# State-space stage of a hybrid trunk: three output tiles as one group, and more filling ahead of the decay products

## The chip, the cores and the metric

The kernel runs on one core of a Trainium2 chip. The metric is the device time of one execution in microseconds. The engines of the core are TensorE (PE; its weight loads are PEld), VectorE (DVE), ScalarE (ACT), GpSimd (POOL) and SyncE (SP); each works through its own queue in order, and semaphores join them. TensorE's accumulators lie in PSUM, everything else on the chip in SBUF.

## What is computed

One inference step of two layers on 384 tokens (128 of a prompt, 256 latent ones) with 1024 features, in float32. Layer 0 mixes tokens by state-space heads (SSD) and gated delta heads side by side, then a ConvFFN; layer 1 by spatial gating and windowed attention, then another. The change lies in layer 0's mixer. Of its reference this matters:

```python
def ssd_scan(x, dt, A, Bm, Cm, h0):              # chunks of 128 tokens
    acs = jnp.cumsum(dtc * A.astype(F32), axis=2)
    seg = acs[:, :, :, None, :] - acs[:, :, None, :, :]
    lmat = jnp.exp(jnp.where(tril, seg, -jnp.inf))                 # decay
    xdt = xc * dtc[..., None]
    scores = jnp.einsum('bcihn,bcjhn->bcijh', cc, bc) * lmat
    y_diag = jnp.einsum('bcijh,bcjhp->bcihp', scores, xdt)
    chunk_states = jnp.einsum('bcjhn,bcjh,bcjhp->bchpn', bc, decay_to_end, xdt)
    y_off = jnp.einsum('bcihn,bchpn,bcih->bcihp', cc, h_prev, jnp.exp(acs))
...
y = rmsnorm(y.reshape(bsz, length, SSD_INNER) * jax.nn.silu(z.astype(F32)), ssd_norm_w)
...
mixed = jnp.concatenate([y, o.reshape(bsz, length, DN_V)], axis=-1).astype(h.dtype)
return mixed @ w_out
```

`o` is the delta heads' output, `w_out` the output projection of both.

## The kernel before

**Matmuls in two halves.** Every projection is done with a high and a low half of each operand: ScalarE casts a high half (`whi` of a weight at L345, `oh`, `hh` of an activation at L371), and VectorE or GpSimd subtracts it from the source to make the low half (`wlo` at L348, `ol`, `hl` at L372). A tile of 128 output features takes eight contraction rows k and three matmuls for each (high by high, low by high, high by low), 24 in all. `Net.group` (L393, L395) and `Net.acc` (L378 to L380) write them, the latter in one order for each k and without a loop over tiles. Four PSUM banks serve these tiles. Weights come in an order planned beforehand, through three landing buffers `wst` and six pairs of halves.

**Weaving.** The mixer's scans have little matmul work between long chains on the other engines. So they are written as generators that yield a pair (TensorE's work just issued, the time to wait before the next piece), and `weave` fills the time to wait with pieces of another generator, the filling: it keeps a clock that adds up the planned work, in units of about a microsecond, and takes filling as long as no scan is due. In the delta stage (some 70 to 145 us) the filling is projection tiles. In the state-space stage (some 380 to 530 us) it is first the eight tiles of the SSD input (`fill_x`), with a convolution of five taps on ScalarE (L696) and VectorE (L700), transposes back to tokens (L728), and then the output projection's delta half, `fill_o`; after each of its pieces comes a piece of a modulation "quad" (L301, L308). The compiler's scheduler can shift instructions on each engine; dependences hold.

**Decay.** `decay` makes the exponentials of the sums `seg` for four heads at a time by matmuls (L818) of a triangle with products `er` of a mask and the factors, high half on VectorE, low half on GpSimd (both L809). Pairs of products are made `deep` steps ahead; then a wait of 2.0 units is yielded before the first matmul. `ner`, the number of `er` buffers, is 4 in the state-space stage and 5 in the delta stage, so that `deep` is 2 in both. The buffers also hold the tiles `m` of L1134 and L1135.

**State-space chunk.** For each of three chunks and two halves of the heads: decay; `G` by matmul (L1122), masked to `GU`, `GL` (L1129, VectorE); for each of eight heads a scaled copy on ScalarE (L1134) and a multiply-add on VectorE (L1135); the product with the decay (L1138, VectorE); the state's part (L1150, L1156 to L1160); the output matmuls (L1168, L1171); skip term and gate `z` (L1176, L1177, VectorE; `z` is loaded by GpSimd's queue at L1174), a square on ScalarE (L1179) and its sums (L1183). Beside them run the chunk states: `BT` transposed (L1214), copied (L1217), `xd` made on VectorE (L1221), multiplied (L1225) and added (L1237) or copied out (L1230, through a buffer shared with `z`).

**`fill_o`** splits the delta output (eight casts L371 on ScalarE, eight subtractions L372 on GpSimd), then makes one tile after another with `group`; the copy of a tile to `part` is on ScalarE. `HOLD` = 2 of its pieces are kept for behind the weave.

## Time and profile before

| | |
|---|---|
| three timed runs | 1443.51, 1444.91, 1444.94 us |
| median | 1444.91 us |
| profiled execution, its own time | 1436.85 us |
| its span in the trace | 1435.1 us |
| mean granted clock of TensorE | 0.983 |
| TensorE busy | 1368.8 us (95%) |
| VectorE busy | 929.1 us (65%) |
| ScalarE busy | 791.1 us (55%) |
| GpSimd busy | 196.6 us (14%) |

The profiled execution is one of its own, and all times within the trace are told from its span's start. Durations of single instructions come from it; its own time is what they add up against.

### The profile page before, as it was taken

How to read it: one execution, taken by the hardware profiler on the slowest of the kernel's cores; microseconds unless marked ns; L12 is line 12 of the kernel's file. 1: busy time of each engine (PE TensorE's matmuls, PEld its weight loads, DVE VectorE, ACT ScalarE, POOL GpSimd, SP SyncE). 2: the span in 40 equal slices, each digit the busy share in tenths (PEclk: the TensorE clock that was granted, in tenths of full speed). 3: DMA queues.
4: the chain of work that ended last, by engine and by line, in shares of the span. 5: the costliest groups of instructions: out<-in, count | busy, mean ns of one | idle time of the engine just before them, and what ended most of it. 6: DMA issues, size and time to landing. Idle time of an engine off the chain costs nothing.

```text
span 1435.1 us, 26679 instructions
## 1 busy us (share of the span) xinstructions
PE 1368.8 (95%) x10421; PEld 1297.3 (90%) x10421; DVE 929.1 (65%) x1819; ACT 791.1 (55%) x1757; POOL 196.6 (14%) x189
## 2 busy tenths in 40 slices
PE   5989998999999999899999999999999899999996
PEld 3889897998887789899999998989999899999996
DVE  3586994755889766776676445466667586776432
ACT  3568567668575435655454445454855465555431
POOL 0023011012345304200000113000003300000001
PEclk9999999999999999999999999999999999999998
DMA  9334544302743475645534442544234344344441
GB/s 345 136 117 135 180 156 146 129 29 80 226 150 105 144 243 176 235 136 162 175 119 125 121 125 71 173 145 134 75 118 154 126 120 131 121 129 121 129 122 55
DMA packets 60334, 201.61 MB, mean 140 GB/s; under 512 B 7120, under 2 KB 12000, under 8 KB 60208
## 3 DMA queue, kind: packets, MB, share of 16 engines
q1 hardware_dynamic: 52832, 186.25, 40.8%
q10 hardware_dynamic: 6048, 8.93, 1.7%
q0 software_dynamic: 1328, 4.73, 1.1%
q8 instruction: 82, 1.34, 0.4%
q14 instruction: 44, 0.36, 0.1%
HBM read 191.20 MB, written 8.68 MB: 139 GB/s over the span
## 4 chain that ended last, share of the span: by engine, by line
PE 82%; DVE 8%; POOL 3%; DMA 3%; ACT 2%; issue 2%; SPq 0%; POOLq 0%; DVEq 0%; ACTq 0%
PE mm L393 19%; PE mm L378 11%; PE mm L379 11%; PE mm L380 11%; PE mm L395 10%; PE pmod L301 3%; DVE wlo L348 1%; PE ps L498 1%; DMA wst<-w 1%; POOL er L809 1%; PE mmt L1552 1%; PE ps L1627 1%; PE mmt L1553 1%; PE mmt L1554 1%; POOL xres L564 1%
## 5 line engine op out<-in xcount | busy, mean ns | idle before, releaser
L348 DVE TENSOR_TENSOR wlo<-wst,whi 128x512 fp32r<-128x512 f32 (+1 forms) x497 | 345.5, 700 | 204.5 <-ACT whi L345 199.4
L345 ACT CAST whi<-wst 128x512 fp32r<-128x512 f32 (+1 forms) x505 | 304.6, 613 | 287.9 <-PE mm L379 157.4
L393 PE MATMUL mm<-hh,whi 128*128 128x386 f32 x728 | 247.1, 339 | 6.7 <-ACT hh L371 5.8
L393 PE MATMUL mm<-hh,wlo 128*128 128x386 f32 x728 | 244.8, 336 | 0.0
L395 PE MATMUL mm<-hl,whi 128*128 128x386 f32 x728 | 238.6, 338 | 0.3 <-DVE hl L372 0.2
L378 PE MATMUL mm<-hh,whi 128*128 128x386 f32 x552 | 194.9, 353 | 1.7 <-ACT t L1343 1.5
L379 PE MATMUL mm<-hl,whi 128*128 128x386 f32 x552 | 189.2, 343 | 0.9 <-issue 0.9
L380 PE MATMUL mm<-hh,wlo 128*128 128x386 f32 x552 | 188.5, 342 | 0.6 <-DVE wlo L348 0.6
L393 PEld LDWEIGHTS mm<-hh,whi 128*128 128x128 f32 x728 | 136.8, 188 | 9.3 <-ACT hh L371 6.4
L395 PEld LDWEIGHTS mm<-hl,whi 128*128 128x128 f32 x728 | 136.1, 188 | 1.5 <-DVE hl L372 1.4
L393 PEld LDWEIGHTS mm<-hh,wlo 128*128 128x128 f32 x728 | 136.9, 188 | 0.0
L378 PE MATMUL mm<-gh,whi 128*128 128x386 f32 x352 | 119.5, 339 | 0.0
L379 PE MATMUL mm<-gl,whi 128*128 128x386 f32 x352 | 119.3, 339 | 0.0
L380 PE MATMUL mm<-gh,wlo 128*128 128x386 f32 x352 | 118.9, 338 | 0.0
L378 PEld LDWEIGHTS mm<-hh,whi 128*128 128x128 f32 x552 | 104.9, 190 | 9.0 <-issue 4.2
L598 DVE SCALAR_TENSOR_TENSOR t<-mm,vecs,t 128x385 f32<-128x385 f32 x88 | 54.3, 619 | 84.5 <-ACT t L597 84.5
L379 PEld LDWEIGHTS mm<-hl,whi 128*128 128x128 f32 x552 | 105.0, 190 | 1.9 <-issue 1.5
L380 PEld LDWEIGHTS mm<-hh,wlo 128*128 128x128 f32 x552 | 104.5, 189 | 1.0 <-DVE wlo L348 0.9
L700 DVE SCALAR_TENSOR_TENSOR t<-mm,vecs,t 128x384 f32<-128x384 f32 (+1 forms) x152 | 92.2, 611 | 14.1 <-ACT t L694 10.0
L597 ACT ACTIVATE t<-mm,vecs 128x386 f32<-128x386 f32 x88 | 58.9, 673 | 69.7 <-PE mm L395 69.7
L520 POOL TENSOR_TENSOR sums<-sums,t 128x386 f32<-128x386 f32 x36 | 41.4, 1172 | 336.8 <-DVE t L517 280.5
L378 PEld LDWEIGHTS mm<-gh,whi 128*128 128x128 f32 x352 | 66.5, 189 | 0.0
(434 smaller groups left out, 2581.9 us busy)
## 6 DMA issues: line engine op xcount, KB each, us to landing
wmod<-modw_l SPq DMA_DIRECT2D x96, 512.0 KB, 4.4
wst<-up_l SPq DMA_DIRECT2D x88, 512.0 KB, 3.5
wst<-w SPq DMA_DIRECT2D x56, 512.0 KB, 3.8
wst<-wo SPq DMA_DIRECT2D x32, 512.0 KB, 3.9
wst<-down_l SPq DMA_DIRECT2D x32, 512.0 KB, 3.5
wst<-w1f SPq DMA_DIRECT2D x18, 512.0 KB, 3.8
wst<-down_l SPq DMA_DIRECT2D x16, 384.0 KB, 3.1
wst<-w1t SPq DMA_DIRECT2D x10, 512.0 KB, 3.7
```

What stands on the lines that cost most here:

```text
L301: nc.tensor.matmul(acc[32 * c:32 * c + 32, 0:128], self.cond[:, k, :], w[:, o:o + 128], start=(k == 0), stop=(k == 7), tile_position=(0, 3 ...
L345: self.conv_hi = nc.scalar.copy(out=hi[:, 0:m], in_=st[:, o:o + m])
L348: self.conv_lo = eng.tensor_sub(out=lo[:, 0:m], in0=st[:, o:o + m], in1=hi[:, 0:m].bitcast(F32))
L378: mm(ps, wh, xh, start=start, stop=False)
L379: mm(ps, wh, xl, start=False, stop=False)
L380: return mm(ps, wl, xh, start=False, stop=stop)
L393: mm(ps, w[k // 4][p][:, s], hh[:, k, :], start=(k == 0 and p == 0), stop=False)
L395: mm(ps, w[k // 4][0][:, s], hl[:, k, :], start=False, stop=(k == 7))
L520: (nc.gpsimd if i else v).tensor_add(out=acc[:, i, :], in0=acc[:, i, :], in1=p)
L597: nc.scalar.activation(out=cv, in_=ps, func=AF.Identity, scale=cw(1), bias=self.v(f"ffb_l{l}", n))
L598: stt(out=cv[:, 1:T], in0=ps[:, 0:T - 1], scalar=cw(0), in1=cv[:, 1:T], op0=ALU.mult, op1=ALU.add)
L700: nc.vector.scalar_tensor_tensor(out=o, in0=p, scalar=cw(i), in1=o, op0=ALU.mult, op1=ALU.add)
```

## The change

Three edits. In `decay`, `deep` is written as 2 (it was 2 in both stages already), and the wait ahead of the first matmul is 5.0 units instead of 2.0, in the three decays of the delta stage and the six of the state-space stage. `ner` of the state-space stage is 5 instead of 4. In `fill_o` the first three tiles are made together with `acc`: k is the outer loop and the tiles the inner one, with a yield of 1.6 units after each k, and the copies of these tiles come when all are done; the number of pieces taken inside the weave goes from 8 to 13 less `HOLD`, which leaves the same tiles for behind it. As pieces are smaller, quad pieces come closer together.

```diff
--- before.py
+++ after.py
@@ -798,7 +798,7 @@
     def decay(self, out, c, col, nh):
         net, nc = self.n, self.nc
         steps = [(b, d) for b in range(nh // 4) for d in range(2)]
-        deep = self.ner // 2
+        deep = 2
 
         def factors(b, d):
             m = net.c(("le", "ge")[d]).unsqueeze(1).to_broadcast([128, 4, 128])
@@ -810,7 +810,7 @@
             return rs
 
         rs = [factors(*s) for s in steps[:deep]]
-        yield 0.0, 2.0
+        yield 0.0, 5.0
         for j, (b, d) in enumerate(steps):
             if d == 0:
                 ps = net.ps()
@@ -1254,7 +1254,7 @@
         end()
         endb, self.hb = net.open("hb", 2)
         end, self.w = net.open("ssd", 1)
-        self.ner = 4
+        self.ner = 5
         out_tile = self.ssd(A)
         end()
 
@@ -1480,9 +1480,17 @@
             for n in range(8):
                 net.split(oh[:, n, :], ol[:, n, :], oT[:, n, :], nc.gpsimd)
             part.append(A("part"))
+            ws = [net.wload(t["wo0"][n, :, 0:1024], 2 - n) for n in range(3)]
+            pss = [net.mm() for _ in ws]
+            for k in range(8):
+                for ps, w in zip(pss, ws):
+                    net.acc(ps, w, k, oh[:, k, :], ol[:, k, :], k == 0, k == 7)
+                yield 1.6
             for n in range(7):
-                nc.scalar.copy(out=part[0][:, n, :], in_=net.group([t["wo0"][n, :, 0:1024]], oh, ol)[0])
-                yield 3.9
+                ps = pss[n] if n < 3 else net.group([t["wo0"][n, :, 0:1024]], oh, ol)[0]
+                nc.scalar.copy(out=part[0][:, n, :], in_=ps)
+                if n > 2:
+                    yield 3.9
             part.append(net.ps()[:, 0:T])
             open_tile(part[1], net.wload(t["wo0"][7, :, 0:1024]), oh, ol, True)
             yield 3.9
@@ -1503,7 +1511,7 @@
         work = [self.ssd_chunk(c, BT, CT, xD, xtok, S) for c, S in
                 ((0, None), (2, (s1[0], s0[1])), (1, (s0[0], s1[1])))]
         rest = fill_o()
-        fill = mix(chain(self.fill_x(), itertools.islice(rest, 8 - HOLD)), chain(net.quads(0, range(8, 12), net.wst), net.quads(1, range(Q0, Q2), net.wst)), 1)
+        fill = mix(chain(self.fill_x(), itertools.islice(rest, 13 - HOLD)), chain(net.quads(0, range(8, 12), net.wst), net.quads(1, range(Q0, Q2), net.wst)), 1)
         weave([late(g, d) for g, d in zip([states()] + work, DS)], fill, W0[3])
         drain(fill, rest)
         part, hold = part
```

How this moves instructions is seen in their order on each engine. Numbers behind names tell tiles apart and are not the same in both programs; words in brackets are the engines waited for.

**First place: the start of `fill_o` (about 436 us in the trace of before), TensorE and ScalarE.** TensorE before, from the last modulation matmuls into the first output tile:

```order
L301 MATMUL pmod_5165<-wmod_5550,cond_83 32x128 [waits DMAHW1_49]
L301 MATMUL pmod_5165<-wmod_5550,cond_83 32x128 x7
L393 MATMUL mm_5596<-oh_5567,whi_5183 128x386 [waits Activation_49]
L393 MATMUL mm_5596<-oh_5567,wlo_5184 128x386
L395 MATMUL mm_5596<-ol_5568,whi_5183 128x386 [waits Pool_49]
L393 MATMUL mm_5596<-oh_5567,whi_5183 128x386 [waits Activation_49]
```

Now the tiles of `fill_o` are `mm_5466`, `mm_5467` and `mm_5468`, and k = 0 of the first two stands further up (not shown); from there to k = 1:

```order
L728 MATMUL ps_5379<-cst_76,t386_5292 128x128 [waits PE_49,Activation_49]
L728 MATMUL ps_5379<-cst_76,t386_5292 128x128 x2
L308 MATMUL pmod_5138<-cst_76,t386_5419 128x128 [waits Activation_49]
L1225 MATMUL ps_5425<-xd_5423,btok_5421 128x256 [waits DVE_49,Activation_49]
L1225 MATMUL ps_5425<-xd_5423,btok_5421 128x256
L1183 MATMUL ps_4717<-cst_76,yt_5327 128x1 [waits PE_49]
L1183 MATMUL ps_4717<-cst_76,yt_5327 128x1 x3
L1214 MATMUL ps_5434<-cst_76,BC_4707 128x128 x2
L378 MATMUL mm_5466<-oh_5437,whi_5156 128x386 [waits Activation_49]
L378 MATMUL mm_5467<-oh_5437,whi_5253 128x386
L379 MATMUL mm_5466<-ol_5438,whi_5156 128x386 [waits Pool_49]
L380 MATMUL mm_5466<-oh_5437,wlo_5157 128x386
```

Before, the eight k of one tile followed each other; now transposes, an L1225 that wants `xd` and an L1183 stand between k = 0 and k = 1. ScalarE before, with the casts `oh`:

```order
L1373 ACTIVATE xD_4709<-t386_5222,vecs_77 128x386 [waits Activation_49]
L371 CAST oh_5567<-qT_1325 128x386 [waits PE_49]
L696 ACTIVATE t386_5365<-mm_5334,vecs_77 128x386 [waits PE_49]
L371 CAST oh_5567<-qT_1325 128x386
L305 COPY t386_5560<-pmod_5165 128x128 [waits PE_49]
L371 CAST oh_5567<-qT_1325 128x386 x3
L1179 ACTIVATE yt_5281<-xD_4709 128x512 [waits DVE_49]
L371 CAST oh_5567<-qT_1325 128x386 x2
L1134 ACTIVATE er_5304<-GU_5300,dt_697 128x128 [waits DVE_49]
L1134 ACTIVATE er_5304<-GU_5300,dt_697 128x128 x3
L1134 ACTIVATE er_5314<-GU_5300,dt_697 128x128 x4
```

and now, behind the cast of k = 0, which stands 21 rows further up:

```order
L1179 ACTIVATE yt_5327<-xD_4709 128x512 [waits DVE_49]
L1231 DMA ossd<-so_5366 128x512 [waits DMAHW6_49,Activation_49]
L1372 COPY xtok_4710<-ps_5379 128x3x128 [waits PE_49]
L1373 ACTIVATE xD_4709<-t386_5292,vecs_77 128x386 [waits Activation_49]
L305 COPY t386_5419<-pmod_5138 128x128
L1217 COPY btok_5421<-ps_5369 128x256
L1134 ACTIVATE er_5389<-GU_5385,dt_697 128x128 [waits DVE_49,Pool_49]
L1134 ACTIVATE er_5389<-GU_5385,dt_697 128x128 x3
L1134 ACTIVATE er_5399<-GU_5385,dt_697 128x128 x4
L371 CAST oh_5437<-qT_1325 128x386 x7
L345 CAST whi_5458<-wst_5456 128x512 [waits DMAHW2_49]
```

The seven other casts moved behind the eight L1134 of a chunk, which they preceded before.

**Second place: VectorE behind it.** Before:

```order
L1221 TENSOR_TENSOR xd_5295<-xtok_4710,dts_725 128x512
L1129 TENSOR_TENSOR GU_5300<-ps_5274,cst_76 128x256 [waits PE_49]
L1129 TENSOR_TENSOR GL_5301<-ps_5274,cst_76 128x256
L348 TENSOR_TENSOR wlo_5327<-wst_5324,whi_5326 128x512 [waits DMAHW7_49]
L1135 SCALAR_TENSOR_TENSOR er_5304<-GL_5301,dt_697,er_5304 128x128 [waits DVE_49,Activation_49]
L1135 SCALAR_TENSOR_TENSOR er_5304<-GL_5301,dt_697,er_5304 128x128 [waits Activation_49] x2
L700 SCALAR_TENSOR_TENSOR t386_5365<-mm_5334,vecs_77,t386_5365 128x384
L1135 SCALAR_TENSOR_TENSOR er_5304<-GL_5301,dt_697,er_5304 128x128 [waits Activation_49]
L1135 SCALAR_TENSOR_TENSOR er_5314<-GL_5301,dt_697,er_5314 128x128 [waits Activation_49]
L1138 TENSOR_TENSOR Es_4736<-Es_4736,er_5304 128x512 [waits DVE_49]
L1135 SCALAR_TENSOR_TENSOR er_5314<-GL_5301,dt_697,er_5314 128x128 [waits Activation_49] x3
```

and now, from the masks of the chunk to the low half of the third tile's weights:

```order
L1129 TENSOR_TENSOR GL_5386<-ps_5353,cst_76 128x256
L1221 TENSOR_TENSOR xd_5423<-xtok_4710,dts_725 128x512 [waits Activation_49]
L1135 SCALAR_TENSOR_TENSOR er_5389<-GL_5386,dt_697,er_5389 128x128 [waits DVE_49,Activation_49]
L1135 SCALAR_TENSOR_TENSOR er_5389<-GL_5386,dt_697,er_5389 128x128 [waits Activation_49] x3
L1135 SCALAR_TENSOR_TENSOR er_5399<-GL_5386,dt_697,er_5399 128x128 [waits Activation_49]
L1138 TENSOR_TENSOR Es_4736<-Es_4736,er_5389 128x512 [waits DVE_49]
L1135 SCALAR_TENSOR_TENSOR er_5399<-GL_5386,dt_697,er_5399 128x128 [waits Activation_49] x3
L1237 TENSOR_TENSOR s1f_4715<-s1f_4715,ps_5425 128x512 [waits PE_49]
L1138 TENSOR_TENSOR Es_4736<-Es_4736,er_5399 128x512 [waits DVE_49]
L1221 TENSOR_TENSOR xd_5480<-xtok_4710,dts_725 128x512
L348 TENSOR_TENSOR wlo_5459<-wst_5456,whi_5458 128x512 [waits DMAHW2_49,Activation_49]
```

The weight split `wlo` and two `xd` (L1221) now stand around one chunk's L1135 and L1138, and the tap sums L700 are all further up.

**Third place: GpSimd at the first decays of the state-space stage (about 385 to 400 us).** Before:

```order
L348 TENSOR_TENSOR wlo_4752<-wst_4745,whi_4751 128x512 [waits DVE_49,DMAHW6_49,PE_49,Activation_49]
L348 TENSOR_TENSOR wlo_4825<-wst_4818,whi_4824 128x512 [waits DVE_49,DMAHW1_49,PE_49,Activation_49]
L809 TENSOR_TENSOR er_4730<-cst_76,fbl_706 128x512 [waits PE_49]
L809 TENSOR_TENSOR er_4734<-cst_76,fbl_706 128x512 [waits PE_49]
L1463 DMA BC_4707<-bd_602 128x8x386 [waits DMAHW6_49,DMAHW5_49,DMAHW7_49,DMAHW4_49,DMAHW2_49]
L809 TENSOR_TENSOR er_4739<-cst_76,fbl_706 128x512 [waits PE_49]
L809 TENSOR_TENSOR er_4743<-cst_76,fbl_706 128x512 [waits PE_49]
L348 TENSOR_TENSOR wlo_4898<-wst_4891,whi_4897 128x512 [waits DMAHW5_49,DVE_49,Activation_49]
L809 TENSOR_TENSOR er_4791<-cst_76,fbl_706 128x512 [waits PE_49]
```

and now:

```order
L348 TENSOR_TENSOR wlo_4752<-wst_4745,whi_4751 128x512 [waits DVE_49,DMAHW6_49,PE_49,Activation_49]
L348 TENSOR_TENSOR wlo_4804<-wst_4797,whi_4803 128x512 [waits DVE_49,DMAHW1_49,PE_49,Activation_49]
L1463 DMA BC_4707<-bd_602 128x8x386 [waits DMAHW5_49,DMAHW7_49,DMAHW4_49,DMAHW2_49]
L809 TENSOR_TENSOR er_4730<-cst_76,fbl_706 128x512 [waits PE_49]
L809 TENSOR_TENSOR er_4734<-cst_76,fbl_706 128x512 [waits DVE_49,PE_49]
L348 TENSOR_TENSOR wlo_4877<-wst_4870,whi_4876 128x512 [waits DMAHW5_49,Activation_49]
L348 TENSOR_TENSOR wlo_4956<-wst_4949,whi_4955 128x512 [waits DMAHW0_49,PE_49,Activation_49]
L809 TENSOR_TENSOR er_4739<-cst_76,fbl_706 128x512 [waits PE_49]
L809 TENSOR_TENSOR er_4743<-cst_76,fbl_706 128x512 [waits PE_49]
L809 TENSOR_TENSOR er_4844<-cst_76,fbl_706 128x512 [waits PE_49]
```

The load of `BC` and two weight splits moved ahead of products that they followed, or that had none before them.

## Rows read from the trace of the kernel before

**Rows 1.** the page, busy time of each engine over the whole span

```profile
PE 1368.8 (95%) x10421; PEld 1297.3 (90%) x10421; DVE 929.1 (65%) x1819; ACT 791.1 (55%) x1757; POOL 196.6 (14%) x189
```

**Rows 2.** TensorE's waits, 76 to 92 us: waited for, us in total, times, longest

```profile
PE ps L818 <- DVE er L809: 2.4, 2, 1.8
```

**Rows 3.** the same view of TensorE's waits, 384 to 436 us

```profile
PE ps L818 <- POOL er L809: 2.3, 3, 1.7
```

**Rows 4.** the same view of TensorE's waits, 436 to 530 us

```profile
PE mm L395 <- POOL ol L372: 2.4, 2, 1.8
...
PE ps L818 <- POOL er L809: 2.1, 1, 2.1
```

**Rows 5.** windows: stretch, busy us of PE, PEld, DVE, ACT, POOL, granted clock, DMA share, GB/s

```profile
384.00:392.00 8.00, 6.31 (x46) 5.36 (x38) 6.23 (x10) 2.47 (x5) 5.20 (x5) 1.00 0.62 192
...
436.00:452.00 16.00, 13.62 (x75) 11.68 (x65) 15.37 (x23) 9.99 (x25) 14.89 (x12) 0.79 0.36 116
...
484.00:492.00 8.00, 5.72 (x37) 4.13 (x36) 5.73 (x12) 2.22 (x5) 5.67 (x5) 1.00 0.41 123
```

**Rows 6.** TensorE's timeline, 429 to 455 us: start, duration, and idle before it

```profile
429.56 1.10 PE L1225 MATMUL ps<-xd,btok 128*128 128x256 f32 x4 [0.34 <-DVE xd L1221]
...
436.42 0.44 PE L393 MATMUL mm<-oh,whi 128*128 128x386 f32 x1
...
446.51 0.35 PE L395 MATMUL mm<-ol,whi 128*128 128x386 f32 x1
...
446.69 0.34 PE L393 MATMUL mm<-oh,whi 128*128 128x386 f32 x1
...
447.26 0.27 PE L308 MATMUL pmod<-cst,t 128*128 128x128 f32 x1
...
451.60 1.08 PE L1225 MATMUL ps<-xd,btok 128*128 128x256 f32 x4
...
452.52 0.95 PE L1183 MATMUL ps<-cst,yt 128*128 128x1 f32 x8
...
453.59 1.03 PE L1150 MATMUL ps<-s1f,BC 128*128 128x256 f32 x4
```

**Rows 7.** ScalarE's timeline, 427 to 437 us

```profile
427.65 0.67 ACT L696 ACTIVATE t<-mm,vecs 128x386 f32<-128x386 f32 x1
...
430.30 2.45 ACT L1134 ACTIVATE er<-GU,dt 128x128 f32<-128x128 f32 x8 [1.98 <-DVE GU L1129]
...
436.33 0.50 ACT L371 CAST oh<-qT 128x386 fp32r<-128x386 f32 x1
```

**Rows 8.** GpSimd's timeline, 435 to 445 us

```profile
435.94 8.28 POOL L372 TENSOR_TENSOR ol<-qT,oh 128x386 fp32r<-128x386 f32 x6 [10.53 <-ACT oh L371]
```

**Rows 9.** VectorE's timeline, 429 to 461 us

```profile
429.33 0.61 DVE L700 SCALAR_TENSOR_TENSOR t<-mm,vecs,t 128x384 f32<-128x384 f32 x1
...
437.80 0.41 DVE L1129 TENSOR_TENSOR GU<-ps,cst 128x256 f32<-128x256 f32 x1
...
450.28 1.22 DVE L1221 TENSOR_TENSOR xd<-xtok,dts 128x512 f32<-128x512 f32 x1
...
457.78 3.02 DVE L809 TENSOR_TENSOR er<-cst,fbh 128x512 fp32r<-128x512 f32 x2
```

**Rows 10.** the view of the tile z on GpSimd's queue, 440 to 500 us

```profile
DMA to landing us min/median/max: 3.4/4.0/4.9
```

**Rows 11.** VectorE's groups by line, 420 to 438 us: busy us, mean ns | idle before

```profile
L1135 DVE SCALAR_TENSOR_TENSOR er<-GL,dt,er 128x128 f32<-128x128 f32 x16 | 5.2, 370 | 0.0
...
L1138 DVE TENSOR_TENSOR Es<-Es,er 128x512 f32<-128x512 f32 x4 | 3.6, 912 | 0.0
...
L1221 DVE TENSOR_TENSOR xd<-xtok,dts 128x512 f32<-128x512 f32 x3 | 2.0, 676 | 0.0
```

**Rows 12.** VectorE's groups by line, 438 to 450 us

```profile
L1135 DVE SCALAR_TENSOR_TENSOR er<-GL,dt,er 128x128 f32<-128x128 f32 x8 | 6.4, 847 | 0.6 <-ACT er L1134 0.6
...
L1138 DVE TENSOR_TENSOR Es<-Es,er 128x512 f32<-128x512 f32 x2 | 2.8, 1377 | 0.0
```

## The prediction

> **What bounds the kernel now.** I read the page first: TensorE is busy for 95% of the span and VectorE for 65% [rows 1], so only time in which TensorE stands still, or runs below full clock, can be won. The list of its waits, asked for stretch by stretch, shows where that is in the two places that the change touches. In the delta stage (76 to 92 us) two waits for decay products of VectorE make 2.4 us, the longest 1.8 [rows 2]. In the state-space stage three waits for decay products of GpSimd make 2.3 us between 384 and 436 us, the longest 1.7 [rows 3]; behind 436 one more of these makes 2.1, and two waits of the first output tile for `ol`, the low half of the delta output, make 2.4 [rows 4]. The window around that tile shows the clock too: over 436 to 452 us the granted clock is 0.79, while it is 1.00 in the windows around the two waits on GpSimd [rows 5], which means that part of it ran at the lower of the two levels, 1.2 instead of 2.4 GHz; a fifth of 16 us is 3.4 us.
>
> The timeline gives the same loss in another way. The first matmul of that tile starts at 436.42 us, and the small L308 behind its 21st at 447.26 [rows 6], 10.84 us. In between lie 21 tile matmuls at 0.18 us (446.51 to 446.69), one L1225 pair at 0.92 (451.60 to 452.52) and one set of transposes at about 0.4 (three small ones like L308, 0.27, that overlap) [rows 6]: 5.1 us. **5.7 us** are lost at the start of the group, idle and clock together. With the other waits above, all that the touched stretches could give back is 5.7 + 2.3 + 2.1 + 2.4 = 12.5 us, 0.9% of the time.
>
> **The change, part by part.** It adds no arithmetic: the tiles have the same matmuls in both orders. So the sum consists of waits that go and waits that come.
>
> *The product wait 2.0 to 5.0, delta stage.* TensorE now does 30 matmuls of the next projection tile before it takes the products for which it waited 1.8 us. That stall goes. But the tile after it needs a bank which VectorE clears with its tap sums L700, and these stand on VectorE behind the same products, whose lateness was the stall; only what TensorE's tile covers of them is won. I give back more than half: **−0.8 us**, bounds 0 and −1.8.
>
> *The same, with the fifth buffer, at the start of the state-space stage.* The first of GpSimd's waits goes, 1.7 us [rows 3]. But GpSimd's own order is changed (the third place shown above): two halves of weight splits (L348) and the load of BC now stand ahead of the products that TensorE asks for next, and an instruction of this kind takes GpSimd 1.4 us (8.28 for six, [rows 8]). Bounds −1.7 and +1.1 (two such instructions less the 1.7 won); I take **−0.3 us**.
>
> *The grouped tiles.* Here I walk through the new order from the end of the last input tile, T = 0. Between it and the first L1225 of the group TensorE has 16 matmul rows of the modulation, two L1225 pairs, eight L1168 rows, L1122, L1214, two transpose sets, L308 and the six matmuls of k = 0. The stretch 429.56 to 436.42 of before [rows 6], 6.86 us without an `ol` wait, holds the same but for one L1225 pair (+0.92), the transposes (+0.8), L308 (+0.1) and 11 tile matmuls more (−2.0): TensorE arrives at T = 6.7. That cover does its work: `oh` and `ol` of k = 0 are there.
>
> The L1225 wants `xd` of L1221, though, which stands on VectorE behind 15 operations: four L700, two L1129, eight L1135, two L1138, one each of L1176 and L1177, and an earlier L1221. Before, the same list (with L1237 for one L1221) ran without a pause from 429.33 to the start of the L1129 at 437.80 [rows 9], 8.5 us. It can begin when ScalarE has opened the tap sum, 0.67 us behind the tile [rows 7]. And L1177 multiplies by `z`, whose load GpSimd now issues only after the first `ol`, about T = 1.1; a load lands 4.0 us after its issue [rows 10], some 0.7 us later than VectorE gets there. So `xd` is ready at 0.67 + 8.5 + 0.7 = 9.85: **a wait of 3.1 us**.
>
> The other seven `oh` casts now stand on ScalarE behind eight L1134, which need the GU of VectorE, at about T = 8.3 (L1138, L1129 and L1221 come after it, 1.6 us). Eight L1134 take 2.45 and a cast 0.50 [rows 7], the first `ol` 1.4: k = 1 is complete at 12.6, one more `ol` every 1.4 us. TensorE, after L1225 (0.92), L1183 and L1214 (1.07, 452.52 to 453.59) and two matmuls with `oh`, is there at 12.2, and with 1.1 us of work for each k it waits again at k = 2 and 3: 0.4 + 0.5 + 0.3 = **1.2 us**, until it stands at T = 16.7 before the third tile's low half `wlo`.
>
> That `wlo` is VectorE's, behind eight L1135, two L1138, L1237 and L1221, from T = 9.85. What these cost is the heart of the matter. While GpSimd hardly worked (420 to 438 us) an L1135 took 0.37 us, an L1138 0.91, an L1221 0.68 [rows 11]; while GpSimd made the `ol` (438 to 450) an L1135 took 0.85, an L1138 1.38 [rows 12], and an L1221 then 1.22 [rows 9]; for the split L348 I take 0.85 too. In the new order GpSimd makes `ol` from T = 11 to 21 without a gap, right over this list. I take the low price for the first four L1135 and the high one behind: 4 × 0.37 + 4 × 0.85 + 2 × 1.38 + 0.68 + 1.22 + 0.85 = 10.4, so `wlo` at 20.2 and **a wait of 3.5 us**. By the low price throughout (with L348 as L1221) it is 6.8, `wlo` at 16.7 and no wait. I take the high one, because the shapes, the engine beside them and even the names are the same as in those rows. The Trainium skill (SBUF — State Buffer, "Who interferes with whom") has a rule for it: a VectorE instruction with two SBUF inputs contends with a GpSimd instruction that reads SBUF, and whoever comes second waits for the whole instruction; the two sets of durations above agree with it, and it speaks against this change, which puts GpSimd's longest run over VectorE's list of just such instructions. By the rule the sum is the one below; without it, it is that of the first rival.
>
> Next comes the following `xd`: one more split 0.85, two products L809 (between 0.68, as L1221, and 1.5, half of 3.02 [rows 9]; I take 1.1), L1237 and L1221, T = 24.6; TensorE has L1225, two L1150 pairs (taken as L1225's, of the same shape), L1214 and three matmuls meanwhile, 23.7: **0.9 us**. Together 3.1 + 1.2 + 3.5 + 0.9 = 8.7 us in place of the 5.7: **+3.0 us**.
>
> *Later decays.* The wait of 2.1 us [rows 4] and a small one go, 2.4 together, since the products stand between pieces of tiles. But the loads of `z` for the next halves come behind GpSimd's products, whose buffers the late TensorE frees, and with 4.0 us to land [rows 10] the squares that L1183 sums are late by about 2 us. **−0.4 us**, bounds −2.4 and +2.
>
> *Sum:* −0.8 − 0.3 + 3.0 − 0.4 = **+1.5 us**. Set against the profiled execution that is 1436.85 + 1.5 = 1438.35; that execution lies 8.06 us below the median of the three timed runs, so carried over to the median 1444.91 + 1.5 = **1446.4 us**. A difference below 0.2% (2.9 us) can hardly be told from none in this kernel. Forecast: no change that can be measured.
>
> **The rivals.** *VectorE is not slowed.* If VectorE's list goes at the low price, `wlo` and the next `xd` are there in time: 3.1 + 1.2 = 4.3 us of waits instead of 8.7, the sum is −0.8 − 0.3 − 1.4 − 0.4 = −2.9, 1442.0 us; with the good bounds of the smaller terms it is −7.3. For it: TensorE is the engine with 95%. Against it: the rows from 438 to 450. It decides at an L1135 mean below 0.5 us.
>
> *The change does what a longer cover promises.* No wait takes the place of those removed: −5.7 − 2.4 − 1.7 − 0.8 = −10.6, 1434.3 us. Against it: VectorE was busy for 15.37 of the 16 us from 436 to 452 [rows 5], so what TensorE gains there it must wait for VectorE.
>
> *The clock falls again.* Today 2.4 us of waiting went with a stretch at the lower level that cost 3.4 us [rows 4, 5]. I expect waits of 3.1 and 3.5 us within 17 us. One such stretch over tile matmuls, not over waiting, gives 1.5 + 3.4 = +4.9: 1449.8 us, slower by 0.34%. It decides as soon as more than half of that stretch falls on matmuls that nothing else holds up. Against it: the waits of 1.7 and 2.1 us on GpSimd's products stand in windows whose granted clock is 1.00 [rows 5].
>
> **How the numbers follow.** Forecast 0.42, with its own range of −2 to +3 us; clock falls 0.30; VectorE not slowed 0.20; as promised 0.08. Of the not-slowed case half is faster by over 0.2%, the promised one wholly, and the forecast with its smaller terms at their good bounds adds some: 0.25. The clock case is slower, and the forecast's upper end adds some: 0.33. Left for no change: 0.42. The range goes from 1439.5 (inside the not-slowed case, the promised one left out) to 1452 (the clock case with half of what the bad bounds of the smaller terms add, 0.8 + 1.4 + 2.4).
>
> **What would show it.** In the profile after: in the list of waits the L395 waits for `ol` are gone and L378/L379 wait for `oh` and `ol` instead; L1225 waits for `xd` by some 3 us (nothing there: the walk's first wait is wrong); L380 waits for `wlo` (nothing there: the price of VectorE's list is wrong); L1135 has a mean near 0.8 in the ten us of the `ol`; GpSimd's product waits are below 2 us in all; the granted clock of the group's 16 us tells the third rival. The forecast is wrong if VectorE's work on the state-space products gets ahead of the place where I put it, because then every wait from the first `xd` on shrinks alike.

## The result, and the profile after

The changed kernel takes 1453.47 us, median of four runs (1450.58 to 1456.61), beside 1444.93 for the kernel before on the same chip: a ratio of 1.0061 [1.0035, 1.0087], **8.5 us slower** where 1.5 had been forecast, and outside the range. Its profiled execution is the fastest of the four, 1450.58 us with a span of 1448.8; that of before was a fast one too, 8 us below its median.

The page's busy times of the changed kernel answer to [rows 1]:

```profile
PE 1376.6 (95%) x10421; PEld 1305.0 (90%) x10421; DVE 937.0 (65%) x1819; ACT 788.4 (54%) x1755; POOL 191.7 (13%) x189
```

The instructions of TensorE and VectorE are the same in number, so what changed is waiting, the clock, and how long single instructions take. TensorE's waits in the delta stage (76 to 92 us) answer to [rows 2]:

```profile
PE mm L378 <- DVE t L700: 1.9, 1, 1.9
PE ps L818 <- POOL er L809: 0.7, 2, 0.4
...
PE ps L818 <- DVE er L809: 0.3, 1, 0.3
```

The 1.8 us wait for the product is gone and the tile behind it waits for its bank, for tap sums L700. The prediction had expected this wait to give back more than half of the win; it gave back all of it. Next, from 383 to 440 us, beside [rows 3]:

```profile
PE ps L818 <- DVE er L809: 3.6, 2, 3.3
PE ps L818 <- POOL er L809: 2.0, 2, 1.5
PE ps L1214 <- ACT xtok L1372: 1.1, 1, 1.1
```

Before, 2.6 us had stood here (the 2.3 of [rows 3] and the 0.34 for `xd` in [rows 6]); now there are 6.7, of them 5.6 for products. Then the group, 440 to 475 us, beside [rows 4]:

```profile
PE ps L1150 <- DVE s1b L1237: 2.2, 1, 2.2
PE pmod L308 <- ACT t L305: 1.2, 1, 1.2
PE ps L1225 <- ACT er L1134: 1.1, 1, 1.1
PE ps L1225 <- DVE xd L1221: 0.5, 1, 0.5
```

The third row is a wait for `xd` by its time: it ends at 450.88 us, and VectorE's L1221 runs from 450.05 to 450.73. From 475 to 545 us 1.4 us of waits are left (2.7 before). The windows of four microseconds around the group, beside the second of [rows 5]:

```profile
444.00:448.00 4.00, 4.00 (x43) 3.18 (x41) 3.53 (x10) 2.65 (x7) 0.00 (x0) 1.00 0.65 188
448.00:452.00 4.00, 1.63 (x6) 1.11 (x5) 4.00 (x14) 3.78 (x13) 0.00 (x0) 0.85 0.81 254
452.00:456.00 4.00, 4.00 (x17) 3.82 (x16) 4.00 (x6) 4.00 (x10) 3.54 (x4) 0.50 0.00 0
456.00:460.00 4.00, 3.92 (x18) 3.59 (x17) 4.00 (x5) 0.17 (x1) 4.00 (x4) 0.80 0.01 2
```

The granted clock falls once behind the waits of 448 to 452, and costs 0.15 × 4 + 0.50 × 4 + 0.20 × 4 = 3.4 us, as much as before. The stretch falls on matmuls: from 452 to 456 us TensorE is busy all the time, at half the clock.

VectorE's multiply-adds, from 440 to 452 us and then from 452 to 465 us, where GpSimd makes seven `ol`, answer to [rows 11] and [rows 12]:

```profile
L1135 DVE SCALAR_TENSOR_TENSOR er<-GL,dt,er 128x128 f32<-128x128 f32 x13 | 3.7, 345 | 0.0
```

```profile
L1135 DVE SCALAR_TENSOR_TENSOR er<-GL,dt,er 128x128 f32<-128x128 f32 x4 | 3.5, 908 | 0.0
```

**What made 6.7 us of 2.6.** GpSimd's timeline at the first decays, then VectorE's and TensorE's (in brackets the idle time before a row and what ended it):

```profile
393.95 0.97 POOL L1463 DMA_DIRECT2D BC<-bd  x1 [5.64 <-DMA bd<-t]
394.94 2.06 POOL L809 TENSOR_TENSOR er<-cst,fbl 128x512 fp32r<-128x512 f32 x2
396.95 2.50 POOL L348 TENSOR_TENSOR wlo<-wst,whi 128x512 fp32r<-128x512 f32 x2
399.42 1.03 POOL L809 TENSOR_TENSOR er<-cst,fbl 128x512 fp32r<-128x512 f32 x1
```

```profile
391.97 3.13 DVE L700 SCALAR_TENSOR_TENSOR t<-mm,vecs,t 128x384 f32<-128x384 f32 x5
395.02 5.98 DVE L809 TENSOR_TENSOR er<-cst,fbh 128x512 fp32r<-128x512 f32 x1
400.93 0.68 DVE L348 TENSOR_TENSOR wlo<-wst,whi 128x512 fp32r<-128x512 f32 x1
```

```profile
401.06 0.73 PE L818 MATMUL ps<-er,tri 128*128 128x512 f32 x2 [3.26 <-DVE er L809]
```

This is a queue that works in order. The load of BC, moved ahead of two products, waits for the last store of `bd`, and GpSimd stands behind it for 5.64 us. Then five instructions that have piled up run without a gap from 394.94 to 400.45, and one product of VectorE, started 0.08 us after the first of them, ends only after the last: 5.98 us, where the shortest of this kind here is 0.67. Before, BC waited 1.2 us, GpSimd had pauses, and no product of VectorE took more than 1.57. It speaks against the load's own transfer as the cause that before, it landed 7.4 us after its issue at 389.88, and a product of VectorE that started at 391.53, in the middle of that, took 0.69 us.

A run of GpSimd without a gap isn't enough for such a stall, though. Before, a little later, five products of GpSimd and three of VectorE ran side by side:

```profile
396.85 7.24 POOL L809 TENSOR_TENSOR er<-cst,fbl 128x512 fp32r<-128x512 f32 x5 [1.02 <-PE ps L818]
399.24 3.94 DVE L809 TENSOR_TENSOR er<-cst,fbh 128x512 fp32r<-128x512 f32 x3 [0.42 <-PE ps L818]
```

There each of GpSimd's took 1.42 to 1.50 us and each of VectorE's 1.03 to 1.53: both were slowed and neither stood still for the whole run. What decides between the two patterns isn't known from these runs.

A time for the stage: from the last transposes of the preceding delta solve to the last high-by-high matmul (L378) of the last tile that uses `yh` (248.19 and 568.06 us before, 319.9 us) the changed kernel needs **5.5 us more**. Of the 13.7 us between the two profiled executions the other 8.2 lie ahead of the stage (3.0) and behind it (5.3). As much lies between two profiles of the kernel before (next section), so where the other 3 us of the medians' difference lie can't be read from this pair.

### The profile page after: what moved, and what is told of

The parts are those of the page before. It is cut to its first block, busy times and chain, and to the rows that moved or that the text cites. A ratio compares the mean times of both kernels' runs of the same rounds, so it can differ in the third digit from the quotient of the medians.

```text
span 1448.8 us, 26688 instructions
## 1 busy us (share of the span) xinstructions
PE 1376.6 (95%) x10421; PEld 1305.0 (90%) x10421; DVE 937.0 (65%) x1819; ACT 788.4 (54%) x1755; POOL 191.7 (13%) x189
## 4 chain that ended last, share of the span: by engine, by line
PE 61%; DVE 5%; ACT 1%; issue 1%; POOL 1%; DMA 1%; POOLq 0%; DVEq 0%; ACTq 0%
PE mm L393 19%; PE mm L395 9%; PE mm L378 7%; PE mm L379 7%; PE mm L380 7%; PE pmod L301 2%; PE ps L498 1%; PE ps L1635 1%; DVE er L1135 1%; PE mmt L1560 1%; PE mmt L1561 1%; PE mmt L1562 1%; DVE wlo L348 1%; DVE u L563 1%; PE ps L420 1%
## 5 line engine op out<-in xcount | busy, mean ns | idle before, releaser
L378 PE MATMUL mm<-hh,whi 128*128 128x386 f32 x552 | 196.1, 355 | 4.0 <-DVE t L700 1.9
L378 PE MATMUL mm<-gh,whi 128*128 128x386 f32 x352 | 119.5, 339 | 0.0
L378 PEld LDWEIGHTS mm<-hh,whi 128*128 128x128 f32 x552 | 105.7, 191 | 10.8 <-issue 3.8
L700 DVE SCALAR_TENSOR_TENSOR t<-mm,vecs,t 128x384 f32<-128x384 f32 (+1 forms) x152 | 92.4, 612 | 12.8 <-ACT t L694 8.9
L301 PE MATMUL pmod<-wmod,cond 128*32 128x128 f32 x1536 | 68.0, 299 | 0.0
```

The source lines that it names most:

```text
L301: nc.tensor.matmul(acc[32 * c:32 * c + 32, 0:128], self.cond[:, k, :], w[:, o:o + 128], start=(k == 0), stop=(k == 7), tile_position=(0, 3 ...
L378: mm(ps, wh, xh, start=start, stop=False)
L700: nc.vector.scalar_tensor_tensor(out=o, in0=p, scalar=cw(i), in1=o, op0=ALU.mult, op1=ALU.add)
```

## Experiments

Each is a variant of one of the two kernels. Where a variant adds lines, the numbers behind them shift: L821 is then L818, L1228 and L1233 are L1225, and L1185 is L1177. "Stage" is the length just defined, against the first profile of before. A second profile of **before itself** shows what that can tell:

> The kernel before once more, unchanged, for a second profile. If the first profiled execution was a lucky one, stretches that the change does not touch (146 to 380 us, and all behind 545 us) are longer here by 2 to 5 us each, with more stretches at the lower clock; else they agree within 1 us.

1446.07 us, stage +1.0, and 8 us more in the other stretches (+4.3 up to 250 us, +3.9 behind 568): the first profile was a lucky one, and unchanged stretches vary by some us. The touched places vary too: its waits are 3.4 us at the first decays (2.6 in the first profile) and 3.6 at the group (2.4), and the lower clock costs 1.7 there (3.4).

**Cover without group (e1), group without cover (e2, e3), delta stage alone (e12).**

```diff
e1, from before:  -ner = 4  +ner = 5;  -yield 0.0, 2.0  +yield 0.0, 2.0 if col == 8 else 5.0
e2, from after:   -ner = 5  +ner = 4;  -yield 0.0, 5.0  +yield 0.0, 2.0
e3, from after:   -yield 0.0, 5.0  +yield 0.0, 5.0 if col == 16 else 2.0
e12, from before: -yield 0.0, 2.0  +yield 0.0, 5.0 if col == 16 else 2.0
```

> The kernel before with five factor buffers and the wait of 5.0 in the delta stage and in the first half of each state-space chunk, no grouped tiles; GpSimd's order at the first decays is that of the changed kernel (load of BC and two weight splits ahead of products). Theory 'GpSimd's queue' (some 4 of the loss come from there): slower than before by 3 to 5 us, and TensorE waits for products of about 6 us in all between 390 and 412 us, one VectorE product lasting over 4 us. Rival 'the group alone': within 2 us of before, or faster, and no such product.

> The kernel before with the three grouped tiles and nothing else (wait 2.0, four buffers). Theory 'GpSimd's queue alone': as before or faster, by 0 to 4 us. Theory 'the group' (its start costs some 4.6 us more than before): slower than before by 3 to 6 us, with xd, ol and s1b waits of TensorE of 4 us or more in the 30 us behind the last input tile. If both places count, this and the run with the wait alone add up to about the 8.5 us of the change.

> The changed kernel with the wait back at 2.0 in the state-space stage (5.0 stays in the delta stage; group and five buffers stay). GpSimd's products are ahead of the load of BC again. Theory 'GpSimd's queue': 3 to 5 us faster than the changed kernel, so 4 to 5 slower than before. Rival 'the group alone': as the changed kernel, some 8 us slower than before.

> Kernel before with the longer cover (5.0) and factors computed two steps ahead in the delta stage alone; the decay products of the state-space stage, their buffers (four) and the tiles as before. Theory S: the delta stage changes by 0 to -1.2 us, state-space stage as before: 1444 to 1446.5 (same). Rival (the delta part of the change is itself slow, hidden in the sum): over 1448.

Measured: e1 1458.87 (1.0096 [1.0073, 1.0119]), stage +11.3; e2 1462.33 (1.0116 [1.0094, 1.0138]), stage +11.6; e3 1453.99 (1.0068 [1.0036, 1.0100]), stage +10.6; e12 1446.18 (1.0004 [0.9984, 1.0025]), stage 0.0. The delta part of the change costs nothing and wins nothing. In the state-space stage each half of the change is slow by itself: e1, whose cover isn't quite that of the change since the second halves of the chunks keep 2.0, has the long product (6.05 us), waits 5.1 us from 440 to 475 (2.8 of it for a load of modulation weights at L301) and loses 5.1 there at the lower clock. e2 and e3 lack the long product (none over 1.78, product waits of 2.1 and 3.2 us from 383 to 440) and lose at the group and behind it instead: e2 4.0 us from 440 to 475 and 8.8 from 475 to 545 (2.7 before), e3 7.3, of it 5.6 for one `xd`, and 5.9. So neither half is "the" cause. e1 and e2, 13.3 and 16.8 us slower than before where 3 to 6 had been expected, don't add up to the change.

**The blocked product (e4): BC's load behind six products.**

```diff
-        nc.gpsimd.dma_start(out=BC, in_=...)
+        with self.tc.issue_after(self.last_factor.ins):   # behind the first six products
+            self.load()
```

> The changed kernel with one difference: GpSimd issues the load of BC behind the six first low-half products of the state-space stage, not ahead of four of them. Theory 'GpSimd's queue': the 6 us product of VectorE near 395 us and the waits of 3.3 and 1.5 us of TensorE there are gone, 3 to 5 us faster than the changed kernel (about 4 slower than before). Rival 'the group alone': within 1.5 us of the changed kernel. Third way: the load comes later, and TensorE's L1214 or L1122 waits for BC instead, by 2 us or more.

1456.61 us, 1.0070 [1.0046, 1.0094], stage +8.6. Its waits from 383 to 440 us:

```profile
PE ps L821 <- POOL er L809: 1.6, 4, 0.9
PE ps L1228 <- DVE xd L1224: 0.7, 1, 0.7
PE ps L821 <- DVE er L809: 0.4, 1, 0.4
```

The 6.7 us are 2.7 and no product of VectorE takes over 1.78: that the load's place made the stall is shown. In every run with the load ahead of those products (the changed kernel twice, e1, e5, e9) one product takes 5.03 to 6.05 us, in all others none over 1.79. But the kernel isn't faster. The four microseconds come back at the group, where the waits are 7.1 us instead of 5.0, the longest of them

```profile
450.37 0.47 PE L308 MATMUL pmod<-cst,t 128*128 128x128 f32 x1 [3.04 <-ACT t L305]
```

and around it the clock falls for 6.8 us' worth (3.4 in the changed kernel).

**GpSimd's `ol` (e5, e6, e7).** Only the first of the eight `ol` pieces is made and the matmuls of all k use it, so GpSimd is free while VectorE works; TensorE's work is the same. The low part of seven contraction rows is left out of the result.

```diff
-                net.split(oh[:, n, :], ol[:, n, :], oT[:, n, :], nc.gpsimd)
+                net.split(...) if n == 0 else nc.scalar.copy(out=oh[:, n, :], in_=oT[:, n, :])
```

> The changed kernel, but GpSimd makes the low half ol of k = 0 only and the matmuls use that one for every k (seven subtractions of GpSimd are left out, so the delta output's low part is not the reference's; TensorE's work is the same). Theory 'GpSimd holds VectorE' (an L1135 at 0.85 us instead of 0.3 while ol is made): VectorE's list behind the group's first xd ends some 5 us earlier, the wait in front of the second L1150 (2.2 us) is gone, 3 to 6 us faster than the changed kernel. Rival 'VectorE's list is late by itself, by its place in the order': within 2 us of the changed kernel.

> The kernel before with the same seven subtractions left out. Its two waits for ol (2.4 us) and, if these are what pulls the clock down, the stretch at the lower clock (3.4 us) go: up to 5.7 us faster than before. If VectorE then becomes what TensorE waits for, less than 3 us.

> The changed kernel with the load of BC behind the six products and with the seven subtractions left out. Theory 'given back at the group': what the BC edit wins at the decays (some 4 us of waits) was given back at the group in the run without this second edit; with the group relieved it stays, so this is 3 us or more faster than the run that only leaves ol out. Rival 'the decays were covered anyway': as that run, within 1.5 us.

From the changed kernel (e5): 1452.94, 1.0062 [1.0043, 1.0081]; from before (e6): 1444.20, 0.9985 [0.9964, 1.0007]; from e4 (e7): 1456.99, 1.0073 [1.0046, 1.0100]. Their stages are +4.7, −0.6 and +7.3. In the changed kernel the `ol` are worth half a microsecond. VectorE's list is faster, as expected, and the wait for `s1b` goes, but those for `xd` grow from 1.6 to 2.8, and the lower clock at the group costs 3.4 as in the changed kernel: the rival, within 2 us of the changed kernel, holds. In e6 one wait of 1.8 us for the single `ol` is left of the two. In e7 L308 still waits 3.0.

**Loads of `z` (e9 to e11, e17, e18).** VectorE's L1177 waited 0.5 us (after) and 1.7 (e7) for `z`, whose load stands behind the first `ol`; is that what holds L305 and `xd`?

```diff
+        if c == 1 and b == 0:          # e9 to e11; e17, e18: c == 0
+            z = ...; nc.gpsimd.dma_start(out=z, ...)
         yield from self.decay(E, c, 8 * b, 8)
```

> The changed kernel; the z load of the first half chunk is issued at the start of that half's decays (ahead of its factors on GpSimd) instead of behind the first ol piece. Theory Z (at the group VectorE's and ScalarE's in-order lists are late because z lands late): VectorE's idle of 0.47 us before L1177 goes, TensorE's waits between 440 and 475 us fall from 5.0 to about 4.0, time about 1452.5. Theory S (the loss is the blocked VectorE product at the start of the decays, and the group's xd is late by VectorE's own work): waits at 440 to 475 unchanged, time 1453 to 1455. Either way the 6 us product at 395 us stays.

> As e4 (changed kernel, BC load behind the first six factor products), with the z load early as well. Theory Z: in e4 the 4 us won at the start of the decays were given back since z was late (L308 <- ACT t 3.0, L1225 <- xd 1.3) and the clock fell; now these go, no clock stretch at 448 to 464, time 1444 to 1448. Theory V (VectorE's list, in order, is the bound from the group on, whatever lands early): L308's wait shrinks but L1225's xd and L379's ol waits stay at about 4 us and the clock falls once: 1452 to 1457.

> As e10, and only the first of the seven remaining ol pieces is made (the low-half matmuls of the other input tiles then use the first piece: part of the result is left out in value, not in work on TensorE). Theory Z: with both suspects gone no wait over 1 us at 440 to 475, full clock there, time 1440 to 1446. Theory V: still a wait of 1.5 to 2.5 us for xd, clock half for about 3 us, 1449 to 1456.

These three moved the load of a later half (of the chunk taken third), not the one that the theory speaks of; VectorE waited 2.5, 1.9 and 1.7 us for that. What they did move was the order of the lists, probably because the buffer of `z` is shared with that of the states' copies. e9: 1458.90 (1.0097 [1.0060, 1.0135]), stage +14.7; e10: 1455.86 (1.0072 [1.0049, 1.0094]), +6.4; e11: 1451.42 (1.0039 [1.0015, 1.0062]), −0.4. e9 is slower than either theory had it; e11 fits theory Z by its waits and clock, theory V by its time. The right load came next:

> As e4 (changed kernel, BC load behind the first six factor products), and now the z load of the very first half (chunk 0), which the first L1177 of the group's VectorE list multiplies by, is issued ahead of that half's decays; e9 to e11 had moved the load of a later half (chunk 1) and VectorE still waited 1.9 us for this one in e10. Theory Z: VectorE's wait of 1.7 to 1.9 us before L1177 and TensorE's wait of 3.0 us for L308 (e4) go; from e4's 1456.6 the time falls by 3 to 7 us, to 1449 to 1453. Theory V (VectorE's list, at GpSimd's price, is the bound from the group on): the wait moves to wlo (2 to 4 us), the time stays at 1454 to 1458.

> As e17, with only the first of the remaining ol pieces made (as e5, e7). Theory Z: from e7's 1457.0 it falls by 4 us or more, since there the only late thing in front of the group was z; 1446 to 1452. Theory V with ol's price: it is 3 to 5 us below e17, whatever e17 is. Rival: it stays within 2 us of e7, and then neither z nor ol is what gives back the win at the start of the decays.

e17: 1458.65 (1.0083 [1.0058, 1.0108]), stage +8.3; e18: 1455.25 (1.0062 [1.0039, 1.0085]), +8.5. VectorE doesn't wait for `z` (in e4, against what was expected, it hadn't either; in e7 1.7), and L308 waits 3.0 as in e4 and e7: **the theory of `z` falls.** In e17:

```profile
443.25 0.68 DVE L1185 TENSOR_TENSOR xD<-xD,z 128x512 f32<-128x512 f32 x1
```

```profile
450.68 0.33 PE L308 MATMUL pmod<-cst,t 128*128 128x128 f32 x1 [3.04 <-ACT t L305]
```

ScalarE's timeline tells what does hold it, here of e4:

```profile
447.74 2.43 ACT L1137 ACTIVATE er<-GU,dt 128x128 f32<-128x128 f32 x8
450.08 0.24 ACT L305 COPY t<-pmod 128x128 f32<-128x128 f32 x1
```

and of e11:

```profile
445.86 0.53 ACT L1377 ACTIVATE t<-t 128x386 f32<-128x386 f32 x1
446.29 0.26 ACT L305 COPY t<-pmod 128x128 f32<-128x128 f32 x1
```

The copy that L308 transposes stands behind the eight scalings (L1134, here L1137) of the next half in e4, e7, e17 and e18, and L308 waits 3.0 us in all four; it stands ahead of the next eight in the changed kernel (1.2 us), and in e10 and e11, where L308 doesn't wait. That fits in every profile; a kernel that moves this copy alone was not run.

e10 and e11 make a clean pair for GpSimd's price, since their VectorE lists at the group are the same 23 instructions from the same start. The window of that list in e10 (with the `ol`), then in e11 (without; columns as in [rows 5]):

```profile
449.20:463.60 14.40, 9.21 (x71) 7.67 (x70) 14.37 (x23) 6.65 (x18) 9.13 (x8) 1.00 0.22 71
```

```profile
449.20:458.90 9.70, 8.30 (x69) 7.38 (x68) 9.61 (x23) 6.23 (x17) 1.29 (x1) 1.00 0.18 53
```

With GpSimd busy for 9.13 us VectorE takes 4.7 us longer for it. The list ends with two `wlo` and the start of an `xd`, and TensorE's waits there (440 to 475 us) are, in e10 and in e11:

```profile
PE mm L380 <- DVE wlo L348: 3.2, 1, 3.2
PE ps L1233 <- DVE xd L1229: 1.8, 2, 1.3
PE mm L379 <- POOL ol L372: 0.7, 2, 0.5
```

```profile
PE mm L380 <- DVE wlo L348: 1.0, 1, 1.0
PE ps L1233 <- DVE xd L1229: 0.4, 1, 0.4
```

5.7 against 1.4 us, and 4.4 us between the medians.

**Again (e13, e14, e15), and the cover with the three edits (e16).** The changed kernel once more, e11 twice more, and e1 with the three edits of e11.

> The changed kernel unaltered, a second profile. Its timed runs lie at 1450.6 with mean clock 0.98 and at 1452.7 to 1456.6 with 0.976; the first profile was the fastest. If the causes read from the first profile are the kernel's own, the 6 us product at the start of the decays and the wait of 3 to 4 us behind it come again, the waits of TensorE between 440 and 475 us are 4 to 6 us, and any difference in time lies in stretches at the lower clock. Rival: the waits themselves differ from execution to execution, and the first profile's list was chance.

> The kernel of e11 unaltered, a second profile. Its runs lie at 1443.9 to 1446.2 (4 of 10, clock 0.981 to 0.983) and 1451.2 to 1455.0 (6 of 10, clock 0.974 to 0.978); its profile was one of the first kind. If this profile is of the second kind: theory C (state-space stage's waits are cured, and only stretches of lower clock are drawn by chance) expects the same waits within 1.5 us at 383 to 545 us and 5 to 8 us more lost at the lower clock; theory W (waits come back) expects 4 us or more of waits there.

> The same once more, so that one of the two is likely to be of the slower kind; expectations as for the one before.

> Kernel before with five factor buffers and the longer cover in the delta stage and the first halves (as e1, no group of tiles), with the three edits of e11: BC load behind the first six factor products, z load early, only the first ol piece made after the first. Theory: e1's extra over before (14 us) is made of the same late items, so that with the three edits it falls to that of e11 or below: 1444 to 1452. Rival: without the group the waits at the tiles stay (the first tile's 24 products want whi, wlo and xd within 5 us), time 1455 to 1459 as e1.

e13: 1454.61 us, stage +7.0. The long product is there again (5.76 us) and the wait behind it (3.2); the lower clock costs 1.7 us right behind that stall, where the first profile had none, and 1.7 at the group. The group's waits are 6.7 us: 1.5 for `wlo` beside the rows shown. e14: 1443.12, stage +2.7; e15: 1449.68, +1.6. Their waits at the group are 1.4 and 1.5 us, as in e11: there the cure stays. At the decays it doesn't reach as far: from 383 to 440 us e11, e14 and e15 wait 4.5, 5.8 and 5.7 us, of it 1.9 to 2.6 for one product of VectorE. What differs between e14 and e15 lies behind the stage: from 540 to 910 us the lower clock costs 6.8 us in e14 and 12.0 in e15 (6.8 in both profiles of before, 10.2 and 13.7 in those of the changed kernel, 10.2 in e11, but 13.7 in e6 and e12 too, whose stages are as long as that of before). e16: 1454.51 (1.0065 [1.0043, 1.0087]), stage +6.1; from e1's 1458.87 the edits win 4.4 us, no more: the expected 1444 to 1452 is missed, with 3.1 us of waiting for a product of VectorE at 383 to 412 and 3.1 for L1200's `ydg` later.

## Why the prediction was wrong

- **The step that failed** is "The same, with the fifth buffer, at the start of the state-space stage": −0.3 us, bounds −1.7 and +1.1. The waits there went from 2.6 to 6.7 us, +4.1. (Between the second profiles, e8 and e13, they went from 3.4 to 6.0, and the lower clock behind the stall cost 1.7 more.) The prediction had seen the load of BC move ahead of the products and priced what stands on GpSimd by its duration, 1.4 us an instruction. It didn't price the wait of the load itself (5.64 us for the store of `bd`), and the contention that it reckoned with at the group it left out here, where the piled-up run blocks a product that TensorE wants at once. e4 shows that the load's place makes the stall: with the load behind the products the waits are 2.7. It doesn't show that the kernel is slow for this alone: e4 takes 1456.61 us, and loses at the group what it wins here. So adding up the places as if each stood for itself failed as well.
- **The grouped tiles**, +3.0 us, came out at +2.7, but not by the walk's terms. The waits at 440 to 475 us are 5.0 us (forecast 8.7), and the lower clock costs 3.4, where the walk has none. The 5.7 us lost before were 2.4 of waiting and some 3.4 of clock, so it comes to 5.0 + 3.4 − 5.7 = +2.7; in e13 to 6.7 + 1.7 − 5.7 = +2.7 too.
- **VectorE's list** was priced right: `wlo` was ready 19.9 us behind the last input tile (T = 0 at 440.12 us), in e13 20.0, forecast 20.2. But TensorE, forecast to stand there from T = 16.7, came at 19.8 (18.5 in e13), later by its lower clock above all, so the wait of 3.5 us for `wlo` became lost clock: nothing of it is left in the first profile, 1.5 us in e13. The group's `xd` was awaited 1.1 us, not 3.1 (another 0.5 went to an earlier one): it came at T = 10.6 instead of 9.85, but TensorE's own work up to there took 7.9 us, not 6.7, and L308 held it for 1.2, a wait that the walk hasn't. The seven casts began 1 us later than forecast (451.87 us, against T = 8.3 + 2.45 for the eight L1134 ahead of them). The last wait was 2.2 us, not 0.9, for `s1b`, directly ahead of the next `xd` in VectorE's list. That these differences nearly cancel is luck.
- **What the price was worth.** Little here: in e5, without seven of the `ol`, `wlo` is ready at T = 17.6, yet waits of 4.0 us and 3.4 us at the lower clock remain. In e10 against e11 it is worth 4.3 us. The Trainium skill (SBUF — State Buffer, "Who interferes with whom") calls what VectorE and GpSimd share an exclusive lock. VectorE's longer times beside GpSimd in e10 agree with it; the 5.98 us go beyond a wait for one instruction of the other engine, since VectorE's product was held for five.
- **Delta stage**, −0.8: the waits from 76 to 92 us went from 3.1 to 3.4 us, +0.3: 2.0 goes at VectorE's products, 1.9 comes for L700 and 0.3 for GpSimd's products. By the time e12 can't tell it from none.
- **Later decays**, −0.4: 2.7 us of waits became 1.4, −1.3.
- **Rivals.** "VectorE is not slowed" falls with the durations (an L1135 of 0.91 us beside the `ol`); e5, which comes near its condition, has waits of 4.0 us, close to its 4.3, and isn't faster. "Does what a longer cover promises" falls with the result. "The clock falls again" came at the group by its own sign, since its stretch lies on matmuls; but it took the place of the wait for `wlo` and didn't come on top. In e4, e7, e17 and e18, where L308 waits 3.0 us, the lower clock cost 5.1 to 6.8 there.
- **The sum** of the state-space parts is 4.1 + 2.7 − 1.3 = +5.5, and the stage grew by 5.5 (7.0 in e13, with its 1.7 of clock behind the stall).
- **Left open.** By the medians it is 8.5. Between the second profiles it is 8.5 too, 6.0 of it in the stage and 2.6 behind it, where nothing was changed. There the lower clock cost 3.4 and 6.8 us more in the changed kernel's profiles than in those of before, but e6, e11, e12, e14 and e15 show that this comes and goes without the change and with one and the same kernel. Whether the changed kernel draws more of it, and why, isn't settled: the kernel of e11 is slower than before by its median too, with a stage of −0.4 to +2.7 us in three profiles. Nor is it shown which order of the lists would keep both the win at the decays and the group: none of the versions run with cover or group in the state-space stage beats the kernel before by its median.

## What to carry to other kernels

A longer cover doesn't only give an engine more time, it changes what stands ahead of what in every in-order queue; look in each for an instruction that waits for something late, a load above all, and price its wait and what piles up behind it, not its duration. Before grouping work on the engine that is the bound, ask whether the next busiest engine can serve the group: in the changed kernel VectorE was busy for 31.5 of the 32 us from 436 to 468, and a stall cured ahead of that list came back at the group (e4). And take a second profile of an unaltered kernel before explaining a few microseconds.

## What the runs showed of the hardware

- One VectorE product with both inputs in SBUF took 5.98 us (5.76 in the second profile) beside five GpSimd instructions without a gap, 0.67 alone. GpSimd's five weren't slowed: the products took 1.03 to 1.06 us each (1.04 at 470.07 us, with VectorE idle), the two `wlo` 1.29 and 1.25, as short as any on GpSimd in this trace. In another run of five, before, both engines were slowed instead: 1.42 to 1.50 us for GpSimd's products, 1.03 to 1.53 for VectorE's.
- The time of unaltered code varies: two profiles of the kernel before lay 4.3 us apart up to 250 us, and in two profiles of the kernel of e11 the lower clock cost 6.8 and 12.0 us from 540 to 910 us.
